# Two layers of a hybrid trunk: where a quarter of the FFN's up weights is loaded to, and which engine makes three low parts

## The chip, the cores and the metric

The kernel runs on one core of one Trainium2 chip. The metric is device time in microseconds of one execution. TensorE (PE in the profile) multiplies, PEld loads its weights; VectorE (DVE), ScalarE (ACT) and GpSimd (POOL) do the elementwise work, SyncE (SP) issues nearly all loads, and POOL issues DMAs that add to what lies in the destination.

## The reference, cut to what matters

Each of two layers is a mixer (three kinds of attention, left out here) and then this feed-forward part, for 512 prompt frames and 64 sample frames, 576 token columns in all:

```
gu = xn @ w_up                    # xn (576, 1024), w_up (1024, 2 * 2816)
g, u = gu[..., :D_FF], gu[..., D_FF:]
c = conv_b + causal 3-tap depthwise convolution of g with conv_w
h = gelu(c) * u
x = x + h @ w_down                # w_down (2816, 1024)
```

All of it is fp32. The change touches only how `w_up` is brought in and prepared for 18 of the 22 column tiles of each layer.

## The kernel before, in words

**Products.** Every fp32 operand is split into a high part, rounded to TensorE's fp32r form, and a low part, the rest. A product is three matmuls: high by high, high by low, low by high. Making the two parts of a weight block costs a ScalarE copy (the high part) and a subtraction (the low part). The helper `low` makes it in one of two ways. By VectorE it is one TENSOR_TENSOR. With `by_dma` it is a ScalarE copy of the negated high part into the place, and then a POOL DMA that adds the block to it (L1361).

**FFN tiles.** The 2816 columns are 22 tiles f = 0 to 21 of 128 columns. Tiles 0 to 3 (`ffn_f`) are ordinary. Tiles 4 to 21 (`NORD` = 4; `unit_f`) treat the gate columns and the up columns of the tile as one 2 x 2 block product and use seven products in place of eight. The gate's two halves of 512 rows are A11 and A12, the up columns' halves are A21 and A22. VectorE makes four sums of 128 x 512 elements: P = A21 + A22, R = A21 + A11, Q = P + A11, V = Q + A12. A21 itself is not multiplied. `unit_f` runs the products in the order A11, P, R, A12, Q, A22, V, each 12 matmuls of 288 columns, 84 in a tile. The two convolution steps of the tile and its gelu follow (`conv_steps`, tile `c`), and one or more pieces of the down product (`md`) stand between two tiles on PE.

**Preparing a tile's weights.** The generator `wforms` goes over f = 4 to 21. It loads A21 (L1409), A11 and A12 together (L1411) and A22 (L1415), lets 6 us of planned time pass, and has VectorE make P and R. Then it starts `wparts` for the groups a (A11, A12), b (P, R), d (A22), makes Q and V, and starts group c (Q, V). A21 and the sums P and R share the tile r1: A21 is loaded to its second half, P is written to the first half, and R over A21. r1, r0 (A11, A12) and the tile of Q and V are taken in turn from three places (tag `raw`). So r1 of tile f can be loaded only when the low parts of P and R of tile f - 1 are made, and r0 when those of A11 and A12 are. These conditions are waits of SP's queue, which is in order: what stands behind a waiting load waits too. Among these are the down weights (`dr`, L1438), which `down_own` loads.

In `wparts`, group a's low parts are made by VectorE for f up to 9 and by DMA from f = 10 on. Those of b and c are always made by VectorE, and that of d (A22) always by DMA.

**Order.** The program is written by a planner on the host: generators are stepped by a clock that adds up assumed costs, and each engine gets its instructions in the order in which the generators issue them. Engines run that order strictly; a VectorE instruction that waits for a load holds all VectorE work behind it. The tag `of` has two places. In this stage the convolution's tile `c` alone uses them; outside it the norms and the attention outputs do.

In the trace the weights' tiles are called `wr`, the low parts `wlo0{f}a`, `el0{f}b`, `wlo0{f}c`, `el0{f}d`, the high parts `whi...` and `eh...`, the products `m0f{f}A` (A11, A12 and A22), `m0f{f}P` (P and Q), R and V. The first digit is the layer, so `wlo110a` is layer 1, tile 10. Each layer goes through the same order.

Of the kernel before, what the change touches and what calls it, by code (L numbers as in the profile page):

```python
# [14 lines left out]
ALU = mybir.AluOpType  # L15

P = 128
D = 1024
# [24 lines left out]
NORD = 4  # L43
# [4 lines left out]
def trunk_kernel(ctx: ExitStack, tc: tile.TileContext, a: dict, o: dict):  # L48
    nc = tc.nc
    dma = nc.sync.dma_start  # L50
# [30 lines left out]
    def ofw(nm, w=TOK):  # L81
        return ap_.tile([P, GW], F32, tag="of", name=nm, bufs=2)[:, 0:w]
# [57 lines left out]
    vector = Engine(nc.vector, "DVE", dve_cost)  # L140
# [11 lines left out]
    def spawn(label, g, first=False):  # L152
        gens.insert(0 if first else len(gens), [label, g, cx["t"]])
# [30 lines left out]
    def pause(ns):  # L184
        cx["t"] = clk["PE"] + ns
        yield

    def until(cond):
        while not cond():
            cx["t"] = clk["PE"] + 1  # L190
            yield
# [1000 lines left out]
    def layer(l):  # L1192
# [65 lines left out]
        def ffn_f(f):  # L1258
# [27 lines left out]
            def fin():  # L1286
# [8 lines left out]

            chunk(f"g{nm}", a["w_up"][l][:, f * P:(f + 1) * P], ND, act, evg, pre_ev=pre,
                  pre=begin_ffn if f == 0 else (lambda: spawn("wf", wforms())) if f == NORD - 1 else None, norm=[1] if f == 0 else None,
                  post=lambda: (spawn(f"c{l}{f}", conv()), spawn("forms", forms()) if f == 0 else None))

# [56 lines left out]
        def low(out, src, hi, by_dma):  # L1356

            if by_dma:
                scalar.activation(out, hi.bitcast(F32), AF.Copy, scale=-1.0)
                charge("POOL", 900)  # L1360
                nc.gpsimd.dma_start(out, src, accum_op=ALU.add)  # L1361
            else:
                vector.tensor_tensor(out, src, hi.bitcast(F32), op=ALU.subtract)
# [4 lines left out]
        def half_tile(nm, dt=F32):  # L1368
            return slot(nm, dt)[:, 0:512].rearrange("p (k c) -> p k c", k=4)

        def wparts(f, nm, forms_, src, by_dma, small):

            if f > NORD:
                yield from until(lambda: all((f - 1, n) in used for n in forms_))
            elif nm == "a":
                yield from until(lambda: "last" in fast)
            elif nm in "cd":
                yield from until(lambda: "go" in fast)
            yield
            key = f"{l}{f}{nm}"  # L1380
            if small:
                pairs = [(half_tile(f"eh{key}{j}", F32R), half_tile(f"el{key}{j}", F32R))
                         for j in range(len(forms_))]
            else:
                h_, l_ = (wp.tile([P, 8, P], F32R, tag=t, name=f"{t}{key}", bufs=2) for t in ("whi", "wlo"))
                pairs = [(h_[:, 4 * j:4 * j + 4, :], l_[:, 4 * j:4 * j + 4, :]) for j in range(2)]
            for j, n in enumerate(forms_):
                hi, lo = pairs[j]
                scalar.copy(hi, src[:, 4 * j:4 * j + 4, :])
                yield  # L1390
                low(lo, src[:, 4 * j:4 * j + 4, :], hi, by_dma)
                ws[f, n] = (hi, lo)
                made.add((f, n))
                yield

        def wforms():

            w = a["w_up"][l]
            rr = lambda t: t.rearrange("(k p) c -> p k c", p=P)
            for f in range(NORD, NF):  # L1400
                gc, uc = w[:, f * P:(f + 1) * P], w[:, F + f * P:F + (f + 1) * P]

                def raw(i, *need):
                    if f > NORD:
                        yield from until(lambda: all((f - 1, n) in made for n in need))
                    return wp.tile([P, 8, P], F32, tag="raw", name=f"wr{l}{f}{i}", bufs=3)

                r1 = yield from raw(1, "P", "R")
                dma(r1[:, 4:8, :], rr(uc[0:D // 2]))  # L1409
                r0 = yield from raw(0, "A11", "A12")  # L1410
                dma(r0, rr(gc))  # L1411
                if f > NORD:
                    yield from until(lambda: (f - 1, "A22") in made)
                a22 = half_tile(f"wr{l}{f}3")
                dma(a22, rr(uc[D // 2:D]))  # L1415
                yield from pause(6000)
                vector.tensor_tensor(r1[:, 0:4, :], r1[:, 4:8, :], a22, op=ALU.add)
                yield
                vector.tensor_tensor(r1[:, 4:8, :], r1[:, 4:8, :], r0[:, 0:4, :], op=ALU.add)
                yield  # L1420
                spawn("wa", wparts(f, "a", ("A11", "A12"), r0, f > NORD + 5, False), True)
                spawn("wb", wparts(f, "b", ("P", "R"), r1, False, True), True)
                spawn("wd", wparts(f, "d", ("A22",), a22, True, True), True)
                q = yield from raw(2, "Q", "V")
                vector.tensor_tensor(q[:, 0:4, :], r1[:, 0:4, :], r0[:, 0:4, :], op=ALU.add)
                yield
                vector.tensor_tensor(q[:, 4:8, :], q[:, 0:4, :], r0[:, 4:8, :], op=ALU.add)
                yield
                spawn("wc", wparts(f, "c", ("Q", "V"), q, False, False), True)
# [575 lines left out]
```

## Time and profile before

| | |
|---|---|
| median of 3 runs | 2158.13 us (2154.2 to 2158.68) |
| the profiled execution | 2157.9 us |
| its span, first to last instruction | 2156.1 us |
| PE, DVE, ACT, POOL busy | 97%, 70%, 56%, 18% of the span |
| mean granted TensorE clock | 0.992 |

The profiled execution is 1.8 us longer than its span, and 0.2 us under the median. Busy PE time includes matmuls at a lower clock. In the rows of windows the five engines stand in the order PE, PEld, DVE, ACT, POOL, each with its count of instructions, and PEclk is the granted share of TensorE's full clock; each window there runs from the end of one tile's products to the end of the next's, so it holds the down pieces between them. In rows in order of time the bracket gives the idle time just before the instruction and what ended it.

### The profile page before, as it was taken

How to read it: one execution, taken by the hardware profiler on the slowest of the kernel's cores; microseconds unless marked ns; L12 is line 12 of the kernel's file. 1: busy time of each engine (PE TensorE's matmuls, PEld its weight loads, DVE VectorE, ACT ScalarE, POOL GpSimd, SP SyncE). 2: the span in 40 equal slices, each digit the busy share in tenths (PEclk: the TensorE clock that was granted, in tenths of full speed). 3: DMA queues.
4: the chain of work that ended last, by engine and by line, in shares of the span. 5: the costliest groups of instructions: out<-in, count | busy, mean ns of one | idle time of the engine just before them, and what ended most of it. 6: DMA issues, size and time to landing. Idle time of an engine off the chain costs nothing.

```text
span 2156.1 us, 40054 instructions
## 1 busy us (share of the span) xinstructions
PE 2097.5 (97%) x15479; PEld 2057.5 (95%) x15479; DVE 1513.8 (70%) x3176; ACT 1216.1 (56%) x2465; POOL 386.0 (18%) x587
## 2 busy tenths in 40 slices
PE   8999999999999989999999999999999998899998
PEld 7999999999999879999999999999999998899998
DVE  7886657767467877777778766577765587777775
ACT  5656776555535544555556677755554364455554
POOL 2111121111121101112111122201102121121112
PEclk9999999999999999999999999999999999999999
DMA  7443222323233625655343222233323354256552
GB/s 216 117 141 89 73 78 87 89 80 97 84 120 86 150 74 129 150 133 123 114 129 109 81 73 73 73 96 95 103 71 123 88 125 104 77 135 152 134 115 75
DMA packets 343401, 229.63 MB, mean 107 GB/s; under 512 B 13552, under 2 KB 323762, under 8 KB 343146
## 3 DMA queue, kind: packets, MB, share of 16 engines
q1 hardware_dynamic: 325898, 194.88, 30.8%
q0 software_dynamic: 17312, 32.18, 8.3%
q8 instruction: 122, 2.00, 0.4%
q14 instruction: 69, 0.57, 0.1%
HBM read 176.54 MB, written 25.83 MB: 94 GB/s over the span
## 4 chain that ended last, share of the span: by engine, by line
PE 85%; DVE 8%; DMA 2%; issue 2%; ACT 2%; POOL 1%; SPq 0%; DVEq 0%; ACTq 0%; POOLq 0%
PE md L146 8%; PE mo L146 4%; PE mg1b L146 2%; PE mg1a L146 2%; PE mg0a L146 2%; PE mg0b L146 2%; PE mg1c L146 2%; PE mg0c L146 2%; DVE x L117 1%; PE mb1a L146 1%; PE mb0a L146 1%; PE mv1b L146 1%; DMA wr<-in_w_up 1%; PE mv0b L146 1%; PE mv1c L146 1%
## 5 line engine op out<-in xcount | busy, mean ns | idle before, releaser
L117 DVE TENSOR_TENSOR wr<-wr,wr 128x512 f32<-128x512 f32 x144 | 98.6, 687 | 62.4 <-DMA wr<-in_w_up 61.4
L117 DVE TENSOR_TENSOR x<-md,x 128x288 f32<-128x288 f32 x224 | 97.8, 452 | 27.3 <-PE md L146 26.9
L146 PE MATMUL mo<-ml,whio 128*128 128x288 f32 x256 | 75.7, 296 | 0.8 <-DVE ml L117 0.8
L146 PE MATMUL mo<-mh,whio 128*128 128x288 f32 x256 | 75.7, 296 | 0.0
L146 PE MATMUL mo<-mh,wloo 128*128 128x288 f32 x256 | 75.5, 295 | 0.0
L146 PE MATMUL md<-hh0f,dl 128*128 128x288 f32 x240 | 70.8, 295 | 0.6 <-DVE dl L117 0.6
L146 PE MATMUL md<-hl0f,dh 128*128 128x288 f32 x240 | 70.9, 295 | 0.0
L146 PE MATMUL md<-hh0f,dh 128*128 128x288 f32 x240 | 70.8, 295 | 0.0
L146 PE MATMUL md<-hh1f,dl 128*128 128x288 f32 x240 | 70.8, 295 | 0.0
L146 PE MATMUL md<-hl1f,dh 128*128 128x288 f32 x240 | 70.8, 295 | 0.0
L146 PE MATMUL md<-hh1f,dh 128*128 128x288 f32 x240 | 70.8, 295 | 0.0
L117 DVE TENSOR_TENSOR dl<-dr,dh 128x512 fp32r<-128x512 f32 (+1 forms) x72 | 42.9, 596 | 10.9 <-ACT dh L117 10.9
L146 PEld LDWEIGHTS mo<-ml,whio 128*128 128x128 f32 x256 | 48.1, 188 | 1.2 <-DVE ml L117 1.2
L117 ACT ACTIVATE xhf<-x,pcol 128x576 fp32r<-128x576 f32 x16 | 12.4, 778 | 63.9 <-DVE x L117 63.9
L146 PEld LDWEIGHTS mo<-mh,whio 128*128 128x128 f32 x256 | 48.2, 188 | 0.1
L146 PEld LDWEIGHTS mo<-mh,wloo 128*128 128x128 f32 x256 | 48.2, 188 | 0.0
L146 PEld LDWEIGHTS md<-hh0f,dl 128*128 128x128 f32 x240 | 45.2, 188 | 0.8 <-DVE dl L117 0.8
L146 PEld LDWEIGHTS md<-hh1f,dh 128*128 128x128 f32 x240 | 45.2, 188 | 0.0
L146 PEld LDWEIGHTS md<-hl1f,dh 128*128 128x128 f32 x240 | 45.2, 188 | 0.0
L146 PEld LDWEIGHTS md<-hl0f,dh 128*128 128x128 f32 x240 | 45.2, 188 | 0.0
L146 PEld LDWEIGHTS md<-hh1f,dl 128*128 128x128 f32 x240 | 45.1, 188 | 0.0
L146 PEld LDWEIGHTS md<-hh0f,dh 128*128 128x128 f32 x240 | 45.1, 188 | 0.0
(2892 smaller groups left out, 9441.3 us busy)
## 6 DMA issues: line engine op xcount, KB each, us to landing
wr<-in_w_up SPq DMA_DIRECT2D x72, 256.0 KB
wr<-in_w_up SPq DMA_DIRECT2D x36, 512.0 KB
dr<-in_w_down SPq DMA_DIRECT2D x48, 256.0 KB
wro<-in_w_out SPq DMA_DIRECT2D x16, 512.0 KB
xspill<-x SPq DMA_DIRECT2D x16, 288.0 KB
x<-xspill SPq DMA_DIRECT2D x16, 288.0 KB
wrg0a<-in_w_in SPq DMA_DIRECT2D x8, 512.0 KB
wrg0b<-in_w_in SPq DMA_DIRECT2D x8, 512.0 KB
```

The source lines that it names most:

```text
L117: return f(*args, **kw)
L146: nc.tensor.matmul(out, lhsT=lhsT, rhs=rhs, start=start, stop=stop, skip_group_check=True)
```

## The change

A21 gets a place of its own: a tile of tag `of`, 512 of its columns wide, which the convolution's tiles `c` otherwise use. Its load stands first in the round of tile f and asks for no condition on tile f - 1's low parts. r1 is taken only after the 6 us pause, just before the sums, and both sums that use A21 read it from the new place. So the three `raw` places are now taken in the order r0, r1, Q/V. Two low parts go from DMA to VectorE: those of A11 and A12 in tile 10, and that of A22 in tile 4.

```diff
-                r1 = yield from raw(1, "P", "R")
-                dma(r1[:, 4:8, :], rr(uc[0:D // 2]))
+                a21 = ofw(f"wr{l}{f}4", 512).rearrange("p (k c) -> p k c", k=4)
+                dma(a21, rr(uc[0:D // 2]))
                 r0 = yield from raw(0, "A11", "A12")
                 dma(r0, rr(gc))
                 if f > NORD:
...
                 a22 = half_tile(f"wr{l}{f}3")
                 dma(a22, rr(uc[D // 2:D]))
                 yield from pause(6000)
-                vector.tensor_tensor(r1[:, 0:4, :], r1[:, 4:8, :], a22, op=ALU.add)
+                r1 = yield from raw(1, "P", "R")
+                vector.tensor_tensor(r1[:, 0:4, :], a21, a22, op=ALU.add)
                 yield
-                vector.tensor_tensor(r1[:, 4:8, :], r1[:, 4:8, :], r0[:, 0:4, :], op=ALU.add)
+                vector.tensor_tensor(r1[:, 4:8, :], a21, r0[:, 0:4, :], op=ALU.add)
                 yield
-                spawn("wa", wparts(f, "a", ("A11", "A12"), r0, f > NORD + 5, False), True)
+                spawn("wa", wparts(f, "a", ("A11", "A12"), r0, f > NORD + 6, False), True)
                 spawn("wb", wparts(f, "b", ("P", "R"), r1, False, True), True)
-                spawn("wd", wparts(f, "d", ("A22",), a22, True, True), True)
+                spawn("wd", wparts(f, "d", ("A22",), a22, f > NORD, True), True)
```

## Rows read from the trace of the kernel before

**Rows 1.** Tile-to-tile windows: us; five engines' busy us; PEclk; DMA share; GB/s.

```profile
737.31:755.32 18.01, 15.11 (x110) 14.41 (x109) 14.59 (x29) 8.14 (x18) 1.44 (x5) 1.00 0.34 88
755.32:772.50 17.18, 14.98 (x111) 14.40 (x110) 12.70 (x24) 8.14 (x18) 1.84 (x5) 1.00 0.36 93
772.50:793.59 21.09, 16.77 (x111) 16.19 (x109) 13.59 (x25) 8.24 (x18) 1.77 (x5) 0.84 0.33 88
793.59:813.72 20.13, 16.54 (x110) 15.95 (x109) 14.22 (x25) 8.55 (x18) 1.84 (x5) 0.92 0.34 92
813.72:832.89 19.17, 17.78 (x134) 17.54 (x133) 15.03 (x27) 8.67 (x18) 2.19 (x5) 1.00 0.36 97
832.89:854.75 21.86, 19.35 (x134) 19.12 (x133) 14.88 (x27) 13.70 (x28) 6.19 (x8) 0.92 0.50 115
854.75:872.27 17.52, 17.52 (x134) 17.52 (x133) 13.23 (x25) 10.27 (x21) 3.06 (x9) 1.00 0.61 136
...
1798.46:1816.93 18.47, 16.31 (x110) 15.93 (x109) 13.30 (x25) 8.14 (x18) 1.44 (x5) 0.91 0.33 87
```

**Rows 2.** PE in time: start, us, instruction, idle before and its releaser.

```profile
734.12 0.29 PE L146 MATMUL m0f4A<-fh,eh04d 128*128 128x288 f32 x1
...
744.36 0.40 PE L146 MATMUL m0f5A<-fh,wlo05a 128*128 128x288 f32 x1 [2.17 <-DVE wlo05a L117]
...
842.23 0.40 PE L146 MATMUL m0f10A<-fh,wlo010a 128*128 128x288 f32 x1 [2.51 <-DMA wlo010a<-wr]
...
1791.18 0.29 PE L146 MATMUL m1f4A<-fh,eh14d 128*128 128x288 f32 x1
...
1793.90 0.40 PE L146 MATMUL m1f4A<-fh,el14d 128*128 128x288 f32 x1 [2.30 <-DMA el14d<-wr]
...
1804.41 0.40 PE L146 MATMUL m1f5A<-fh,wlo15a 128*128 128x288 f32 x1 [2.16 <-DVE wlo15a L117]
```

**Rows 3.** Waits of DVE over the span: us in total, times, longest.

```profile
DVE wr L117 <- DMA wr<-in_w_up: 61.4, 27, 4.6
```

**Rows 4.** DVE in time: the sum P of tiles 5, 8 and, layer 1, 5, 8.

```profile
736.71 0.69 DVE L117 TENSOR_TENSOR wr<-wr,wr 128x512 f32<-128x512 f32 x1 [0.61 <-DMA wr<-in_w_up]
...
793.97 0.69 DVE L117 TENSOR_TENSOR wr<-wr,wr 128x512 f32<-128x512 f32 x1 [1.32 <-DMA wr<-in_w_up]
...
1794.63 0.69 DVE L117 TENSOR_TENSOR wr<-wr,wr 128x512 f32<-128x512 f32 x1 [1.47 <-DMA wr<-in_w_up]
...
1855.18 0.69 DVE L117 TENSOR_TENSOR wr<-wr,wr 128x512 f32<-128x512 f32 x1 [0.94 <-DMA wr<-in_w_up]
```

**Rows 5.** SP's queue in time: tile 8's three loads (two down loads left out).

```profile
785.49 0.38 SPq L1409 DMA_DIRECT2D wr<-in_w_up  x1
...
787.04 0.41 SPq L1411 DMA_DIRECT2D wr<-in_w_up  x1
787.50 1.22 SPq L1415 DMA_DIRECT2D wr<-in_w_up  x1
```

**Rows 6.** Instructions of the tiles named wr: issue to landing of their loads.

```profile
DMA to landing us min/median/max: 3.2/4.3/7.4
```

**Rows 7.** DVE in time: single instructions of tiles 4, 7 and 10.

```profile
734.32 0.46 DVE L117 TENSOR_TENSOR z0f<-m0f4P,s0f 128x288 f32<-128x288 f32 x1 [3.40 <-PE m0f4P L146]
...
785.38 0.68 DVE L117 TENSOR_TENSOR wlo07a<-wr,whi07a 128x512 fp32r<-128x512 f32 x1
...
836.63 0.68 DVE L117 TENSOR_TENSOR el010b<-wr,eh010b 128x512 fp32r<-128x512 f32 x1
...
847.93 0.69 DVE L117 TENSOR_TENSOR dl<-dr,dh 128x512 fp32r<-128x512 f32 x1 [5.18 <-ACT dh L117]
```

**Rows 8.** Windows of the loading of tile 5, layer 1 (columns as in rows 1).

```profile
1784.00:1795.00 11.00, 8.70 (x66) 8.47 (x65) 5.89 (x11) 4.10 (x10) 1.04 (x2) 1.00 0.84 194
```

**Rows 9.** SP and ACT in time: the ordinary down load after tile 21, its reader.

```profile
1025.11 0.38 SPq L398 DMA_DIRECT2D wrd<-in_w_down  x1
...
1039.85 0.42 ACT L117 CAST whid<-wrd 128x256 fp32r<-128x256 f32 x1
```

## The prediction

> **What bounds the kernel now.** I read the page first, then the windows over single FFN tiles, then TensorE's waits inside them, then VectorE's queue and SP's around these. TensorE sets the end, so only what shortens its waits, or the slow time after them, counts. The windows show where it loses time in the stage that the change touches. From tile 11 on a window is gap-free: 17.52 us for one tile and its down piece, all of it busy at clock 1.00. Tile 10, with the same 132 matmuls, takes 21.86 [rows 1]. Tile 9, also with 132, takes 19.17. Tiles 5 to 8 have a shorter down piece (108 matmuls, 17.52 x 108/132 = 14.33 if gap-free) and take 18.01, 17.18, 21.09 and 20.13 [rows 1]. So what can be won lies in tiles 4 to 10 of each layer; the eleven tiles behind them have nothing to give.
>
> In tile 10 TensorE waits 2.51 us for a low part that is made by DMA [rows 2]. [...] In tile 4 of the second layer it waits 2.30 for A22's low part, by DMA as well [rows 2]. In tile 5 it waits 2.17 and 2.16 for a low part by VectorE [rows 2], because VectorE is late. One reason for that is VectorE's queue: it stood 61.4 us, 27 times, before a sum until weights had landed [rows 3]. Where TensorE waits soon after, in tiles 5 and 8, these stalls are 0.61, 1.32, 1.47 and 0.94 us [rows 4]. The stalls of tile 11 and later, most of the 61.4, cost nothing, since TensorE does not wait there.
>
> **The change part by part.**
>
> *A21's place.* In tile 8 the A21 load goes out at 785.49; behind it in SP's queue stand two down loads, the gate load at 787.04 and A22's at 787.50 [rows 5]. The sum P starts at 793.97, when A22 has landed, 6.47 us after that issue; the median of these loads is 4.3 [rows 6]. A21 in its own place need not wait for tile 7's low parts, so it and the two down loads leave before 785. The gate load then waits only for its own place, whose last reader is VectorE's low part at 785.38 + 0.68 = 786.06 [rows 7]. It goes out about 0.9 earlier, and A22 at about 786.6, with fewer bytes in flight. With the median landing, A22 is there at 790.9. VectorE is free for P at 793.97 - 1.32 = 792.65 [rows 4]: the stall is gone, with 1.7 us to spare. Behind P stand R, the add that ends the tile's gate columns, the convolution, and in ScalarE's queue behind that the high part on which TensorE waits, so 1.32 goes through to TensorE. Bounds: 0, if A22 lands no earlier, and 1.32, as nothing else in that stretch moves. I take 1.32 here, 0.94 in the second layer and 0.61 in the first layer's tile 5 [rows 4].
>
> The added wait is that of the A21 load for its place. Its last occupant is an A21 whose sums P and R stand ahead of the low parts on which the load waits today, or a `c` whose tile ended one tile before; either is free sooner than the place it has now. No `c` waits for an A21 yet to be read, as both its readers stand before the next A21 takes a place. Cost 0; at worst the load leaves as late as now.
>
> *Place order.* As r0 is now taken first, the first ordinary down load after tile 21 takes its place, free only when tile 21's low parts by DMA are done. The load goes out at 1025.11 and is read at 1039.85 [rows 9]: 14.74 less 4.3 of landing leaves 10.4 us of cover. Cost 0; once over 10.4 it would delay the last down pieces one for one.
>
> *Tile 4's A22 by VectorE.* Removed: one negating copy and one DMA per layer. Added: one subtraction of 0.68, as its like in tile 7 takes [rows 7]. It is hidden in the 3.40 us that VectorE idles before the tile's Q add [rows 7]. If that cover were gone it would cost 0.68 per layer. In the first layer TensorE does not wait for this part, so nothing is won there. In the second, from the first A22 matmul to the end of tile 5's wait takes 1804.41 - 1791.18 = 13.23; the first layer does the same in 744.36 - 734.12 = 10.24 [rows 2], and in 9.63 once its stall of 0.61 is gone. So this edit and the early load give 13.23 - 9.63 = 3.60 in the second layer, the 2.30, the slow matmuls behind it and the 1.47 together. Bounds: 2.30 (the wait alone) and 3.60. I take 3.60, since the layers run the same order and differ only by these two waits.
>
> The loads around that stall fill the queues: 84% of the DMA engines' time over 11 us [rows 8], and A22's adding DMA is among them. [...]
>
> *Tile 10's A11 and A12 by VectorE.* Removed: two negating copies and two adding DMAs per layer. Added: two subtractions of 0.68. The first can follow the low part of P at 836.63 [rows 7] and is made at about 838.0, or 838.9 if the V sum and an add go first. TensorE stands at it at 842.23 - 2.51 = 839.72 [rows 2], so the whole wait goes, and the slow stretch with it: 4.34, the distance to tile 11's window. At least 21.86 - 19.17 = 2.69 [rows 1], if tile 10 comes to look like tile 9, where VectorE also makes this part and TensorE still waits. I take 4.34 in each layer; the second layer repeats the window of 21.86 within 0.05. The two subtractions (1.36) are covered by the 5.18 us that VectorE then idles [rows 7].
>
> *Clock.* After the change tiles 5 and 8 have one wait of about 2.17 each, like tile 6. With such a wait the first layer's tiles 5 and 6 stay at clock 1.00, and the second layer's tile 5 falls to 0.91 [rows 1]. From the end of its wait that tile takes 12.52 to its end, against 10.96 in the first layer [rows 1, 2]: 1.56 per slow stretch. Three such stretches, tile 8's two and this one, may go: up to 4.7. Or three may come in tiles 5 and 6: down to -4.7. I take half of the three, 2.3.
>
> [...]
>
> **Sum.** 0.61 + 3.60 + 1.32 + 0.94 + 4.34 + 4.34 = 15.15, and 2.3 for the clock: 17.45. From the profiled execution, 2157.9, that gives 2140.5. Its span is 2156.1 with 1.8 around it; the median of the three runs is 2158.13, 0.2 above, so the same sum serves for it.
>
> **The rivals.**
> - *Loads no earlier* (10%): A22 is slowed by what is still in flight, and the stalls of rows 4 stay. Left are tile 10 and the second layer's 2.30: 8.68 + 2.30 = 10.98, 2146.9. For it: 84% of the DMA time is taken [rows 8]. Against: the A21 load and one adding DMA leave that stretch.
> - *Tile 10 becomes tile 9* (8%): VectorE is late there too; 2 x 2.69 in place of 2 x 4.34, 2143.8. Against: in tile 10 its queue has reached P's low part 3.1 us before TensorE needs A11's [rows 2, 7].
> - *The clock falls the wrong way* (4%): 15.15 - 4.7 = 10.45, 2147.5.
> [...]
> - *Nothing comes of it* (7%): A21's place is free only as late as now and VectorE's low parts come as late as the DMA's did: 2157.9.
> - *Slower* (6%): the planner's charges in tile 4 change, and with them the order in VectorE's and ScalarE's queues in tiles 5 to 9. Tile 7 shows what a bad order costs: 21.09 against tile 6's 17.18 with the same work [rows 1], 3.91 a tile. With four tiles that could turn (5, 6, 8, 9) in two layers, 17.45 is lost again at 4.5 of the eight. Three tile numbers in both layers give 6 x 3.91 - 17.45 = +6.0, 2163.9. Against: VectorE idles 3.40 in tile 4 [rows 7], and a clock that waits forgets a moved charge.
>
> **How the numbers follow.** The forecast has 62%, with its own range 2136 to 2145: no slow stretch left in the six places gives 15.15 + 4.7, 2138.1, tile 7 may lose a slow stretch too (1.56), and one term of some 4 us may fail. The 8-in-10 range reaches over the rivals on the same side, 2135 to 2149. Under 0.2%, or 4.3 us, a measurement of this kernel can't tell a change from none. Faster: 62 + 10 + 8 + 4 + 3 = 87%; the same 7%; slower 6%.
>
> **What would show it.** Right: tile 10's windows near 17.5 with no wait for its low part; A22's load of tile 8 out at about 786.6 relative to the old end of tile 7's products at 793.59 [rows 1]; no DVE wait for `wr` before tile 8; no wait for A22 in tile 4. Wrong: a wait for the low part of tile 10 by VectorE, a DVE wait for `wr` in tiles 5 or 8, a changed order in tiles 5 to 9, or slow stretches in tiles that had none.

## The result, and the profile after

The changed kernel takes 2141.70 us (median of 3, 2141.27 to 2144.42) against 2158.13: a ratio of 0.9933, 95% interval 0.991 to 0.9955. The forecast was 2140.5. The profiled execution took 2141.7 with a span of 2139.9, 16.2 us less than before. All medians here are of executions at the usual mean granted clock, 0.989 to 0.999: one of the seven of e1 below took 2304.63 us at a mean clock of 0.833 and is left out.

The page of the changed kernel, its first part (busy us, share of the span, instructions):

```profile
PE 2091.5 (98%) x15479; PEld 2052.8 (96%) x15479; DVE 1516.6 (71%) x3182; ACT 1212.0 (57%) x2459; POOL 383.5 (18%) x581
```

Before, the three counts were DVE x3176, ACT x2465 and POOL x587: six instructions went from ScalarE to VectorE and six issues left POOL, as the diff says. The windows from tile end to tile end, tiles 5 to 10 of layer 0 and then 5 to 8 and 10 of layer 1, in the columns of [rows 1]; the last fence has tiles 6, 7 and 10 of layer 1 before the change:

```profile
735.76:753.08 17.32, 15.06 (x110) 14.44 (x109) 13.93 (x27) 8.14 (x18) 1.45 (x5) 1.00 0.35 92
753.08:770.13 17.05, 14.89 (x110) 14.40 (x109) 12.60 (x24) 8.13 (x18) 1.84 (x5) 1.00 0.36 93
770.13:791.16 21.03, 16.39 (x110) 15.93 (x109) 14.53 (x27) 8.24 (x18) 1.77 (x5) 0.92 0.34 88
791.16:808.25 17.09, 14.92 (x111) 14.43 (x110) 13.13 (x24) 8.56 (x18) 1.84 (x5) 1.00 0.40 109
808.25:827.39 19.14, 17.76 (x134) 17.54 (x133) 15.05 (x27) 8.68 (x18) 2.40 (x5) 1.00 0.36 97
827.39:844.92 17.53, 17.53 (x134) 17.53 (x133) 15.92 (x29) 12.71 (x26) 3.84 (x6) 1.00 0.49 128
...
1784.92:1803.79 18.87, 16.57 (x110) 15.95 (x109) 13.94 (x27) 8.15 (x18) 1.44 (x5) 0.91 0.32 85
1803.79:1822.28 18.49, 16.33 (x111) 15.80 (x109) 12.60 (x24) 8.13 (x18) 1.84 (x5) 0.91 0.33 86
1822.28:1844.47 22.19, 17.56 (x110) 17.10 (x109) 14.54 (x27) 8.23 (x18) 1.77 (x5) 0.85 0.31 84
1844.47:1863.07 18.60, 16.43 (x110) 15.94 (x109) 13.13 (x24) 8.56 (x18) 1.85 (x5) 0.91 0.37 100
...
1882.23:1899.76 17.53, 17.53 (x135) 17.53 (x133) 15.87 (x29) 12.71 (x26) 3.81 (x6) 1.00 0.48 128
```

```profile
1816.93:1834.13 17.20, 15.03 (x110) 14.45 (x109) 12.69 (x24) 8.13 (x18) 1.85 (x5) 1.00 0.36 92
1834.13:1855.15 21.02, 16.36 (x110) 15.89 (x109) 13.60 (x25) 8.24 (x18) 1.77 (x5) 0.92 0.33 88
...
1894.07:1915.90 21.83, 19.29 (x134) 19.05 (x133) 14.91 (x27) 13.69 (x28) 6.22 (x8) 0.92 0.51 115
```

Against [rows 1], in layer 0: tile 5 gave 18.01 - 17.32 = 0.69, tile 8 gave 20.13 - 17.09 = 3.04, and tile 10 gave 21.86 - 17.53 = 4.33. Tile 10 is now as gap-free as tile 11 was. Tiles 6, 7 and 9 moved by 0.13 or less, tile 7 although its PEclk rose from 0.84 to 0.92. In layer 1, tile 10 gives 21.83 - 17.53 = 4.30. Three windows of this layer hold a wait like that of layer 0's tiles 5, 6 and 8, yet they are 1.4 to 1.6 us longer, with PEclk at 0.91. That is the slow stretch. Behind the wait of layer 1's tile 5 the granted clock is 1.00 from 1791.28 to 1792.40, 0.50 from 1792.64 to 1795.76, where the matmuls start 0.24 us apart, and 1.00 again from 1796.00, where they start 0.13 apart; the 0.50 is what is called the lower clock level here.

VectorE's queue in layer 0, the sums P of tiles 5 and 8 and the low parts of tile 10; then its remaining waits for these loads over the span:

```profile
734.46 0.68 DVE L117 TENSOR_TENSOR wr<-wr,wr 128x512 f32<-128x512 f32 x1
...
790.14 0.68 DVE L117 TENSOR_TENSOR wr<-wr,wr 128x512 f32<-128x512 f32 x1
...
831.04 0.68 DVE L117 TENSOR_TENSOR el010b<-wr,eh010b 128x512 fp32r<-128x512 f32 x1
831.64 0.69 DVE L117 TENSOR_TENSOR wr<-wr,wr 128x512 f32<-128x512 f32 x1
832.24 0.68 DVE L117 TENSOR_TENSOR wlo010a<-wr,whi010a 128x512 fp32r<-128x512 f32 x1
```

```profile
DVE wr L117 <- DMA wr<-in_w_up: 8.1, 4, 3.8
```

The sums have no bracket any more: the stalls of [rows 4] are gone, and of the 61.4 us of [rows 3] 8.1 are left, before the sums of tiles 11 and 12, where TensorE does not wait: it is busy in all of 844.92 to 879.90, and in layer 1 in all of 1899.76 to 1934.80. The low part of tile 10's A11 is made at 832.92, one V sum behind P's, and TensorE's first matmul that needs it runs at 834.07 without a wait:

```profile
834.07 0.30 PE L146 MATMUL m0f10A<-fh,wlo010a 128*128 128x288 f32 x1
```

SP's queue at tile 8 (rows in order of time; the down loads are now L1439):

```profile
774.12 0.38 SPq L1409 DMA_DIRECT2D wr<-in_w_up  x1
774.60 0.96 SPq L1439 DMA_DIRECT2D dr<-in_w_down  x2
783.10 0.37 SPq L1411 DMA_DIRECT2D wr<-in_w_up  x1
783.56 0.53 SPq L1415 DMA_DIRECT2D wr<-in_w_up  x1
```

A21 and the two down loads leave 9 us before the gate load instead of in one burst with it [rows 5]. A22 goes out 7.60 us before the end of tile 7's products (791.16); before the change it was 793.59 - 787.50 = 6.09. What the gate load at 783.10 follows is seen in VectorE's queue:

```profile
782.37 0.69 DVE L117 TENSOR_TENSOR el07b<-wr,eh07b 128x512 fp32r<-128x512 f32 x1 [2.77 <-ACT eh07b L117]
782.98 0.69 DVE L117 TENSOR_TENSOR wlo07a<-wr,whi07a 128x512 fp32r<-128x512 f32 x1
```

It leaves when the low part of tile 7's R is done (782.37 + 0.69 = 783.06), before that of A12 is (783.67). The A21 load of the kernel before left at the same event (785.49, 0.03 after that low part). So SP's queue is held until the same low part in both kernels. What changed is what goes out between that and A22: the A21 load, the two down loads and the gate load then (A22 2.04 us later), the gate load alone now (0.50).

### The profile page after: what moved, and what is told of

The parts are those of the page before. It is cut to its first block, busy times and chain, and to the rows that moved or that the text cites. A ratio compares the mean times of both kernels' runs of the same rounds, so it can differ in the third digit from the quotient of the medians.

```text
span 2139.9 us, 40032 instructions
## 1 busy us (share of the span) xinstructions
PE 2091.5 (98%) x15479; PEld 2052.8 (96%) x15479; DVE 1516.6 (71%) x3182; ACT 1212.0 (57%) x2459; POOL 383.5 (18%) x581
## 4 chain that ended last, share of the span: by engine, by line
PE 88%; DVE 8%; ACT 1%; issue 1%; POOL 1%; DMA 0%; SPq 0%; DVEq 0%; ACTq 0%; POOLq 0%
PE md L146 9%; PE mo L146 5%; PE mg1a L146 2%; PE mg1b L146 2%; PE mg0a L146 2%; PE mg1c L146 2%; PE mg0b L146 2%; PE mg0c L146 2%; DVE x L117 1%; PE mb0a L146 1%; PE mb1a L146 1%; PE mv1b L146 1%; PE mv0b L146 1%; PE mv1c L146 1%; PE mq1c L146 1%; PE mg0f L146 1%
## 5 line engine op out<-in xcount | busy, mean ns | idle before, releaser
L117 POOL COPY stc<-gp1f 128x2 f32<-128x2 f32 x44 | 22.6, 575 | 120.2 <-ACT gp1f L117 61.0
```

What stands on the lines that cost most here:

```text
L117: return f(*args, **kw)
```

## The experiments

All are compared with the kernel before, run beside them on the same chip.

| label | what it is | median us | ratio, 95% interval |
|---|---|---|---|
| e1_place_only | A21's place alone | 2150.38 | 0.9968, 0.9956 to 0.9981 |
| e2_low10_only | tile 10's low parts alone | 2150.28 | 0.9964, 0.9950 to 0.9977 |
| e3_low4_only | tile 4's A22 alone | 2154.55 | 0.9983, 0.9975 to 0.9992 |
| e8_lows_only | e2 and e3 together | 2145.20 | 0.9939, 0.9926 to 0.9951 |
| e4_place_late | e1, A21's load at the old point | 2148.96 | 0.9960, 0.9949 to 0.9972 |
| e5_a21_last | kernel before, A21's load third | 2153.30 | 0.9975, 0.9965 to 0.9985 |
| e6_after_again | the changed kernel again | 2142.54 | 0.9928, 0.9915 to 0.9942 |
| e7_a_first | changed kernel, A11 and A12 prepared first | 2118.90 | 0.9815, 0.9802 to 0.9829 |
| e9_a_first_before | kernel before in that order | 2124.00 | 0.9841, 0.9824 to 0.9857 |
| e10_a_first_lows | e8 in that order | 2119.47 | 0.9821, 0.9806 to 0.9835 |

### The three edits one by one (e1, e2, e3, e8)

e1 is the change without its two edits of `spawn` lines. The others are made from the kernel before:

```diff
# e2, and in e8
-  spawn("wa", wparts(f, "a", ("A11", "A12"), r0, f > NORD + 5, False), True)
+  spawn("wa", wparts(f, "a", ("A11", "A12"), r0, f > NORD + 6, False), True)
# e3, and in e8
-  spawn("wd", wparts(f, "d", ("A22",), a22, True, True), True)
+  spawn("wd", wparts(f, "d", ("A22",), a22, f > NORD, True), True)
```

> A21's own place and early load alone; the three low parts stay with DMA. Theory (SP's queue, held by A21's load, made A22 late and so VectorE): the stalls of VectorE before the sum P in tiles 4, 5 and 8 are gone in both layers, tile 10 keeps its window of about 21.9 and its wait of 2.5. Gain 1.5 (tile 4, layer 0, as read in the changed kernel's trace) + 0.6 + 1.3 + 0.9 + up to 1.5 (tile 5, layer 1), about 5 us, plus or minus two slow stretches of 1.6: 2150 to 2155. Rival (the place gives nothing, all comes from the low parts): within 1.5 us of the kernel before.

> Only tile 10's A11 and A12 low parts by VectorE. Theory: tile 10's window falls from 21.86 to 17.5 in both layers, nothing else moves: gain 8.7 us, 2149.4, plus or minus one slow stretch of 1.6. Rival (tile 10 is free only because VectorE no longer stalls in tiles 5 and 8): tile 10 keeps a wait like tile 9's 1.4, gain about 5.4.

> Only tile 4's A22 low part by VectorE. Theory: layer 1's wait of 2.30 before A22's low part goes with its slow stretch (about 1.2), and VectorE's stall before tile 5's sum there (1.47) becomes shorter, as one adding DMA leaves the queues; layer 0 does not move: gain 2.3 to 3.6 us, 2154.3 to 2155.6. Rival (the DMA queues are as full without it, and A22 of tile 5 lands as late): the 2.30 goes but is given back at tile 5, gain under 1.5.

> Both edits of low parts without the place. Theory (the parts of the change add up): 7.5 (tile 10 alone, measured) + 3.2 (tile 4 alone, measured) = 10.7 under the kernel before, 2147. Rival (tile 4's edit and the place share one gain, tile 5 of layer 1): up to 2 us better than the sum, 2145, as without the adding DMA the stall there goes too.

Measured against the 2157.79 of the kernel before, run beside them, e1 gained 7.4, e2 7.5 and e3 3.2: each in the range its theory gave. The intervals of e1 and e3 shut their rivals out. That of e2 (5.0 to 10.8) takes in its rival's 5.4, and there the window decides. With the place alone, tile 8 has no stall and tile 10 is as it was; with tile 10's edit alone, tile 10 is gap-free:

```profile
792.96:810.03 17.07, 14.91 (x111) 14.41 (x109) 13.13 (x24) 8.57 (x18) 1.84 (x5) 1.00 0.40 109
829.18:850.91 21.73, 19.04 (x134) 18.81 (x133) 14.71 (x27) 13.67 (x28) 6.23 (x8) 0.92 0.55 128
```

```profile
832.41:849.96 17.55, 17.55 (x134) 17.55 (x133) 14.18 (x26) 10.96 (x22) 2.39 (x5) 1.00 0.39 106
```

The first fence is e1's tiles 8 and 10, the second e2's tile 10. In e3 VectorE's waits for these loads from tile 4 to tile 8 of layer 0 are a single one, in tile 8:

```profile
DVE wr L117 <- DMA wr<-in_w_up: 1.2, 1, 1.2
```

So the stall of tile 5 is gone there without A21's place; the one thing taken out of the DMA queues there is A22's adding DMA. In layer 1 e3 keeps 0.34 of the 1.47. Of the three edits only the place removes tile 8's stall. The prediction had given layer 0's tile 5 to the place; it belongs to both edits, since either removes it.

The size of tile 8's stall is not fixed either. Up to tile 10 of layer 0, every engine has the same instructions in the same order in e2 as in the kernel before. There A22 lands 6.5 us after its issue, as before, but VectorE is free for the sum P only later, behind a tile 7 of 22.2 us, and the stall is 0.20 (0.34 in layer 1) where [rows 4] have 1.32 and 0.94:

```profile
793.65 0.69 DVE L117 TENSOR_TENSOR wr<-wr,wr 128x512 f32<-128x512 f32 x1 [0.20 <-DMA wr<-in_w_up]
```

e8 took 2145.20 against 2158.38, 13.2 less, where 7.5 + 3.2 = 10.7 was the plain sum. That is the time its rival named, but e8's interval, 10.6 to 16.0, just takes in the sum, and the two terms have intervals of their own. Whether the edits add up exactly stays open. From e8 to the changed kernel (2142.54, run beside it) the place brings 2.7, with intervals that overlap.

### What it was about the place (e4, e5)

```diff
# e4: e1, with the old condition ahead of the load
+ if f > NORD:
+     yield from until(lambda: (f - 1, "P") in made and (f - 1, "R") in made)
  a21 = ofw(f"wr{l}{f}4", 512).rearrange("p (k c) -> p k c", k=4)
# e5: kernel before, A21's load moved
- r1 = yield from raw(1, "P", "R")
- dma(r1[:, 4:8, :], rr(uc[0:D // 2]))
  r0 = yield from raw(0, "A11", "A12")
...
  dma(a22, rr(uc[D // 2:D]))
+ r1 = yield from raw(1, "P", "R")
+ dma(r1[:, 4:8, :], rr(uc[0:D // 2]))
```

> As the place alone, but A21's load is issued at the planner's old point, after P and R of the tile before are planned; on the chip it has nothing to wait for but its place. Theory (it was the wait in SP's in-order queue that cost, not the time at which A21 lands): the gate load and A22 of tile 8 still go out right after VectorE's low part of A11, the stalls stay away, and the time is that of the place alone within 2 us. Rival (it helps that A21's 256 KB are moved before the others): the stalls of 0.6 to 1.5 us come back, and the time lies within 1.5 us of the kernel before.

> The kernel before with A21's load moved behind the tile's other two, no place of its own, low parts as before. Theory: with A21 last, SP's queue no longer holds the gate load and A22 behind the wait for the low parts of P and R; they go out as early as with the place. A21 itself is still late: it goes out after A22 and lands last, some 1 us behind it. In tile 8 that is 786.6 + 0.5 + 4.3 = 791.4, ahead of the 792.65 at which VectorE is free: the stall there goes, 2150 to 2155. Rival (what counts is that all three land, and A21 needs its own place for that): stalls as before, within 1.5 us of the kernel before.

e4 did not do what it was made for. Its A21 load of tile 8, and TensorE's first matmul of tile 7, stand in e4 and then in e1 as follows:

```profile
778.25 0.38 SPq L1411 DMA_DIRECT2D wr<-in_w_up  x1
...
780.34 0.40 PE L146 MATMUL m0f7A<-fh,whi07a 128*128 128x288 f32 x1 [2.71 <-ACT whi07a L117]
```

```profile
776.13 0.38 SPq L1409 DMA_DIRECT2D wr<-in_w_up  x1
...
778.21 0.40 PE L146 MATMUL m0f7A<-fh,whi07a 128*128 128x288 f32 x1 [2.72 <-ACT whi07a L117]
```

In both the load leaves 2.1 us before that matmul. On the chip it follows the sum R of tile 7, the last reader of the place it takes, by 0.03 us in e4 and 0.04 in e1, so the added condition delays nothing. e4 repeats e1 (2148.96 and 2150.38, with intervals that overlap) and says nothing on whether it matters when A21's bytes are moved.

e5 does take the place away. There A21 has no place of its own and is the last of the three to go out, yet tile 8's sum P (794.74) follows the add before it without a wait:

```profile
786.51 0.37 SPq L1409 DMA_DIRECT2D wr<-in_w_up  x1
786.98 0.53 SPq L1413 DMA_DIRECT2D wr<-in_w_up  x1
787.60 0.46 SPq L1415 DMA_DIRECT2D wr<-in_w_up  x1
```

```profile
794.74 0.68 DVE L117 TENSOR_TENSOR wr<-wr,wr 128x512 f32<-128x512 f32 x1
```

The rows are e5's loads in SP's queue (gate, A22, A21) and VectorE's sum P. The gate load again leaves when R's low part is done (786.49), and A22 0.49 after that. e5 took 2153.30 against 2158.38. So the place is one way to the gain and not the only one; what hurt was that A21 and the down loads stood ahead of the other two and went out with them in one burst. e5, like the change, also takes r0's place before r1's. No run has that order without another edit, so its own share is not shown.

### The same program again (e6)

> The changed kernel once more, unchanged. Theory (the same waits come with or without a slow stretch behind them, from one execution to the next): the waits of tiles 5 to 9 stand as in the first trace (2.16 to 2.17 in tiles 5, 6 and 8, 2.72 in tile 7), but the slow stretches lie in other tiles; time 2141.5 plus or minus 3. Rival (a tile's slow stretch is set by its waits): the same five tiles of layer 1 and one of layer 0 are slow again.

The time came again, 2142.54. The windows of tiles 5 and 6 of both layers in e6:

```profile
735.66:754.45 18.79, 16.52 (x110) 15.90 (x109) 13.92 (x27) 8.14 (x18) 1.45 (x5) 0.91 0.32 85
754.45:771.51 17.06, 14.90 (x110) 14.41 (x109) 12.59 (x24) 8.13 (x18) 1.84 (x5) 1.00 0.36 93
1785.94:1804.81 18.87, 16.57 (x110) 15.95 (x109) 13.93 (x27) 8.15 (x18) 1.45 (x5) 0.91 0.31 85
1804.81:1823.18 18.37, 16.21 (x110) 15.69 (x109) 12.59 (x24) 8.13 (x18) 1.85 (x5) 0.91 0.32 86
```

Layer 0's tile 5 is slow now (18.79), where the first trace of the same program had 17.32 at clock 1.00, with the same wait (2.15 in e6, 2.17 in the first). Layer 1's slow tiles are the same ones as in the first trace. So theory and rival each have a part of it: the wait alone does not decide, and one execution is no sample.

### The waits that are left (e7, e9, e10)

```diff
- spawn("wa", ...)
- spawn("wb", ...)
- spawn("wd", ...)
+ spawn("wd", ...)
+ spawn("wb", ...)
+ spawn("wa", ...)
```

Each `spawn` puts its generator at the head of the list, so this order steps A11 and A12 first.

> The changed kernel with the generators of a tile's low parts started in the other order, so that the planner steps A11 and A12 ahead of P and R, and these ahead of A22. Theory (the 2.17 left in tiles 5, 6 and 8 and the 1.4 in tile 9 are VectorE and ScalarE making A22's and P's parts first, though TensorE takes A11 first): ScalarE has A11's high part 1.0 us earlier and VectorE its low part 1.3 to 1.6 earlier; the waits fall to under 1, some slow stretches with them: 2125 to 2134. Rival (the wait only moves to P, whose parts now come later): within 2 us of the changed kernel.

> The kernel before with nothing but the other order of starting a tile's generators (A11 and A12 first), so A21's place and the low parts are as before. Theory (the order and the change are two separate gains: the order takes VectorE's backlog in tiles 5 to 9, the change takes SP's held queue and the DMA-made low parts): the tile 10 wait of 2.5 with its slow stretch and tile 4's wait stay, so the order brings 23.6 (2142.5 less 2118.9) of its own, 2134 to 2138. Rival (with the order right, VectorE has time enough that the change is hidden): within 4 us of the 2118.9 of the changed kernel in that order.

> That order with the two low-part edits, without A21's place. Theory: the place is worth what it was worth without the order, about 2.7 (2145.2 less 2142.5), 2121 to 2123, with a stall of VectorE before the sum P of tile 8. Rival (the stall of tile 8 is now hidden, as VectorE has no backlog behind it): 2118.9 within 1.5.

e7 took 2118.90, 6 us below the range its theory gave. It is 1.85% faster than the kernel before, and 23.6 us faster than the changed one (2142.54). Tiles 5 to 10 of its layer 0:

```profile
736.00:752.67 16.67, 15.04 (x111) 14.44 (x110) 13.75 (x27) 8.36 (x18) 1.80 (x5) 1.00 0.36 95
752.67:768.98 16.31, 15.09 (x111) 14.39 (x109) 13.56 (x26) 8.23 (x18) 2.20 (x5) 1.00 0.37 97
768.98:785.29 16.31, 14.86 (x111) 14.39 (x109) 13.33 (x26) 8.29 (x18) 1.85 (x5) 1.00 0.42 115
785.29:801.86 16.57, 14.85 (x111) 14.39 (x110) 13.86 (x26) 8.78 (x18) 1.85 (x5) 1.00 0.41 112
801.86:819.33 17.47, 17.47 (x134) 17.47 (x133) 16.35 (x31) 11.81 (x24) 2.34 (x6) 1.00 0.44 121
819.33:836.85 17.52, 17.52 (x134) 17.52 (x133) 14.09 (x26) 10.23 (x20) 3.18 (x8) 1.00 0.65 163
```

No window of the FFN tiles is slow (PEclk is 1.00 in these six, and 0.999 in the mean of the execution), tile 9 has become gap-free, and the longest wait left in a tile is 1.3 us, for R's low part. Part of the wait has moved on, as the rival said, though to R and not to P, and it is small.

e9 overturned its theory. The kernel before in that order takes 2124.0, far under the 2134 to 2138 expected and 1.1 over the reach of its rival (2122.9). Tiles 9 and 10 of its layer 0, the second with A11's low part still made by DMA:

```profile
802.28:819.77 17.49, 17.49 (x134) 17.49 (x133) 14.30 (x26) 11.53 (x23) 2.50 (x5) 1.00 0.38 106
819.77:837.25 17.48, 17.48 (x134) 17.48 (x133) 14.32 (x26) 11.64 (x24) 3.26 (x9) 1.00 0.62 140
```

Tile 10 needs no edit there: TensorE no longer waits for the parts that the DMA makes. Of TensorE's waits that the change removes only tile 4's is left, 0.8 in layer 0 and, in this row of PE's waits (us in total, times, longest), 2.6 in layer 1:

```profile
PE m1f4A L146 <- DMA el14d<-wr: 2.6, 1, 2.6
```

So the change that brought 16 us by itself brings some 5 in the better order (2124.0 - 2118.9 = 5.1). e10 lies within 0.6 of e7, with intervals that overlap, as its rival had it, and tile 8 has no stall there: A21's place, worth 2.7 before, brings nothing there that these runs can measure.

## Why the prediction was right

**A21's place.** Right in the main: A21 and the down loads left early, A22 went out earlier, and the stalls of [rows 4] are gone. e5 shows that the loads ahead of A22 were the cost. Wrong was what the gate load waits for. The prediction named the low part of A12, which ends 0.6 us after that of R. It was the low part of R, so A22 came 1.5 us earlier, where 0.9 was forecast. Tile 7 shows this more plainly: its gate load left with A12's low part before the change (load at 766.27, low part done at 766.24) and leaves 3.6 us ahead of it now (760.31, 763.88). e1 and e5, which also take r0 first, have the gate load of tile 8 at R's low part too. So the order of the places, priced only at the end of the layer, moved this load as well. The attribution of tile 5's 0.61 was too narrow (e3), and the 1.32 was the size in one execution (0.20 in e2).

**Tile 4.** In layer 1 the window of the tile's products went from 15.24 to 11.16. By the prediction's own measure, from the first A22 matmul to the end of tile 5's wait, it takes 1791.28 - 1781.73 = 9.55, for 9.63 forecast:

```profile
1781.73 0.30 PE L146 MATMUL m1f4A<-fh,eh14d 128*128 128x288 f32 x1
...
1791.28 0.40 PE L146 MATMUL m1f5A<-fh,wlo15a 128*128 128x288 f32 x1 [2.17 <-DVE wlo15a L117]
```

In layer 0 it was said that nothing is won, as TensorE does not wait for A22's part. The tile's products became 0.73 shorter (11.91 to 11.18): before, its A11 took 0.49 and its R 0.28 more than the 1.59 of the others (0.22 of it a wait for A11's low part that the sum had left out), now none does; why is not shown. In e1, e2, e4, e5 and e9, which keep that DMA, TensorE waits 0.5 to 1.4 for it in layer 0 as well, and e2 (1.4) has the program of the kernel before up to there. That TensorE did not wait was one execution's luck.

**Tile 10.** 4.33 and 4.30 for 4.34 each. The wait of 2.51 is gone and the slow stretch with it: before, the clock granted behind that wait was 0.50 from 842.70 to 846.00 and 1.00 from 847.00 to the end of the tile. The subtraction stood between the two forecasts for it, behind the V sum but ahead of the add, and was in time.

**Clock.** The term that failed. It was to give back 2.3. Layer 0's tile 8 lost its slow stretch (3.04 - 1.32 = 1.7). In layer 1 the stretches of tiles 5 and 8 stayed, and tiles 6 and 7 took one more each (18.49 for 17.20, and 22.19 for 21.02: 2.5 in all). That is 1.7 - 2.5 = -0.8 in place of 2.3. The rate taken from three windows was too low, and one execution does not fix where the stretches fall (e6): the two traces of the same program have layer 0's tile 5 at clock 1.00 in one and 0.91 in the other behind the same wait, while layer 1's slow tiles came again.

**The sum.** 17.45 was forecast and the spans differ by 16.2; that they are so close is partly luck. The clock fell short by 3.1. Against that stand tile 4 of layer 0 (0.73), the other terms together (15.5 for 15.15), and 0.84 by which the first FFN matmul of layer 0 came earlier (659.36 to 658.52), ahead of anything that the change touches.

**The rivals.** None came in full; the clock went a little the way of one (-0.8, where it had -4.7). The slower one, another order in tiles 5 to 9, did not: tiles 6, 7 and 9 of layer 0 keep their windows to 0.13 us. But e7 shows that the order is where most of the time lay. The prediction read tile 7's 21.09 as the price of a bad order and took tile 6's 17.18 for a good one; the good one is 16.31. That the early load holds up tile 4's activations, for which the sum of chances has 3%, no run shows: in the changed kernel TensorE is busy in all of the 16 us up to the end of tile 4's products, in both layers (719.50 to 735.76, 1768.50 to 1784.92).

## What to carry to other kernels

Here a load that waited for its place held every load behind it in its queue, and when it went they followed in one burst: tile 8's A21 load and the four behind it went out within 2.01 us [rows 5]. In a queue like that, look at what stands between the release and the load that is needed first; put the others behind it, or give them a place so that they leave earlier. Before buying a shorter path for a late operand, see whether the engine that makes it works in the order in which its consumer asks: here three swapped lines were worth 23.6 us on top of the change, and 34.7 without it, and hid most of what the change had bought. A wait of 2 us on TensorE should be priced with the slow stretch that may follow it: here 1.3 to 1.6 us, behind 17 of 36 such waits.

## What the runs showed of the hardware

The same wait of 2.12 to 2.18 us in tiles 5 and 6, between gap-free stretches, was counted in nine traces (before, after, e1 to e6, e8), four windows each. In 17 of 36 a stretch at the lower clock level came with it, among them 6 of the 12 of the kernel before, the changed one and e6, whose windows stand above (PEclk 0.91 in the 6, 1.00 in the others); between the windows shown here, of the same tile with and without one, it cost 1.3 to 1.6 us. The prediction had put the share at one in three. Tile 9's wait of 1.4 us brought none in the 18 windows of the same traces, and waits of up to 1.3 us (e7) none in 8 windows of tiles 5 to 8.
